# Seven products instead of eight in two FFN up projections of a two-block transformer kernel

## The chip, the cores and the metric

One core of a Trainium2 chip runs the whole kernel in one launch. The metric is device time in microseconds (us); a kernel's time is the median of its runs. The traces come from one profiled execution each. The engines are named as in the profile: PE (TensorE), PEld (its weight loads), DVE (VectorE), ACT (ScalarE), POOL (GpSimd) and SP (the queue that issues most transfers).

## The reference

Two blocks work on one sequence of 1024 tokens with a model width of 1024, all in float32. The part that matters here is the FFN of each block, whose hidden width is 4096: an up projection, the square of a relu, a down projection.

```python
y = x @ w_out                                    # mixer output, 1024 x 1024
x = x + rms_norm(y, mix_post_norm)
h = rms_norm(x, ffn_pre_norm)
f = jnp.square(jax.nn.relu(h @ w_up))            # 1024 x 4096
x = x + rms_norm(f @ w_down, ffn_post_norm)
```

The second block does the same with w_out_2, w_mlp_in_2 and w_mlp_out_2; its norms and sums are scaled and shifted by a modulation, a vector of 6144 numbers that one matrix (w_ada_2, 1024 x 6144) makes of a condition vector. That matrix is 25 MB, and its product is computed beside the first FFN.

## The kernel before, in words

A float32 product is made of three matmuls. Each operand is split into a rounded part (hi, a copy on ACT) and the rest (lo, a subtraction on DVE), and `mm3` (L170) adds hi·hi, hi·lo and lo·hi in one PSUM bank. A weight block of 128 x 128 stands still, 512 tokens stream: these are the 128x512 matmuls of L172.

The stage before each FFN is `out_projection`: it computes the mixer output in two halves of 512 tokens. Behind each half, for each tile of 128 tokens, `epilogue` adds the residual, and `norm_to_hT` norms the tile, transposes it on PE (L283) and writes hi and lo of the transposed activations h, 8 blocks of 128 features by 1024 tokens.

`ffn_up` then goes through the 4096 hidden columns in 16 slabs of 256. `w_cols` loads a slab's weights (1 MB, one raw buffer), casts them (L202) and subtracts (L208) into w_hi and w_lo, of which there are two buffers each. For each half of the tokens and each 128 columns there is one product over all 8 feature blocks: 2 x 2 x 8 x 3 = 96 matmuls. ACT takes relu out of PSUM (L977) and squares it (L978). The four results of a slab, f11, f12, f21 and f22 (half, column block), are combined by DVE into five sums (L993), and these and f11 and f22 go to memory in HBM (fs_dr). The down projection reads them from there: it is already computed by seven Strassen products, its weight sums made on POOL (L1034).

Beside the first `ffn_up` runs the modulation. `modulation_acc` loads a 512-column strip of w_ada_2 in four chunks of 512 KB, issued from POOL's queue (L1095), and adds them up on DVE with the condition vector's entries as scalars (L1099, L1101). There are 12 strips, so 48 chunks.

The program text gives dependences; a scheduler that simulates the program with its own costs fixes one order of instructions per engine, and each engine runs its order without overtaking. Buffers are named in `TAGS`, where a number behind a star says how many a name has: "fp" holds those of `ffn_up` and the modulation.

```python
"fp": "f00*4 f01*4 f10 f11 fs4 fs5 fs0 fs1 fs6 ada_acc*2 ada_raw*3 f_r",
```

Of the kernel before, what the change touches and what calls it, by code (L numbers as in the profile page):

```python
# [65 lines left out]
def tile_two_blocks(ctx: ExitStack, tc: tile.TileContext, I, out):  # L66
# [90 lines left out]
    mix_dr = scratch("mix", (D, S))  # L157
    fs_dr = [scratch(f"fs{i}", (P, 16 * 512)) for i in range(7)]
# [110 lines left out]
    def norm_to_hT(t, xt, xn, junk, hh, hl, row=None, gain=None, bias=None, tmp_pool=None):  # L269
# [9 lines left out]
        for g in range(2):  # L279
# [4 lines left out]
            if row is not None:  # L284
                split(hh[:, ks, tok], hl[:, ks, tok], pt.rearrange("p (a b) -> p a b", a=4))
            else:
                tm = tmp_pool.tile([P, 4, P], F32, name="hmod")
                for j in range(4):
                    k = 4 * g + j
                    ACT.activation(tm[:, j, :], pt[:, j * P:(j + 1) * P], AF.Identity,  # L290
                                   scale=gain[:, k:k + 1], bias=bias[:, k:k + 1])
                POOL.tensor_scalar(hh[:, ks, tok], tm, 1.0, 1.0, ALU.mult, ALU.mult)  # L292
                DVE.tensor_tensor(out=hl[:, ks, tok], in0=tm, in1=r32(hh[:, ks, tok]), op=ALU.subtract)

    def new_hT(pool):
        return (pool.tile([P, KT, S], F32R, name="h_hi"), pool.tile([P, KT, S], F32R, name="h_lo"))

# [629 lines left out]
    def epilogue(t, y, gbc, ep, xsrc, xdst, nxt, eng=DVE):  # L927
# [11 lines left out]
        if nxt is not None:  # L939
            nxt(t, xt, y, junk)  # L940

    def out_projection(w, src, y, mxp, after, last):
        for half in range(2):
# [9 lines left out]
            for c in range(4):  # L953
                ws = w_cols(w, 256 * c, 256)
                for tt in range(4):
                    ps = mm_tile(256)
                    tok_major(ps, 0, ms[tt], ws)
                    ACT.copy(y[:, 4 * half + tt, 256 * c:256 * (c + 1)], ps)
            res = last() if half else None
            for tt in range(4):  # L960
                after(4 * half + tt)
# [4 lines left out]
    def ffn_up(h, w_up, fp, first, side=lambda c: None):  # L966
        NC = w_up.shape[1] // 256
        fs, uw = {}, dict(enumerate(first))

        def up(c, half):  # L970
            if c not in uw:
                uw[c] = w_cols(w_up, 256 * c, 256)
            for j in range(2):
                ps = mm_tile()
                feat_major(ps, j * P, halves[half], h, uw[c])
                f = fs[c, half, j] = fp.tile([P, 512], F32, name=f"f{half}{j}")
                ACT.activation(f, ps, AF.Relu)  # L977
                ACT.activation(f, f, AF.Square)  # L978
                if half == 0 or j == 1:
                    if half != j:  # L980
                        continue
                    left(c, 2 if half == 0 else 3, f, ACT)
# [4 lines left out]
        def sums(c):  # L987
            f11, f12, f21, f22 = (fs.pop((c, half, j)) for half in range(2) for j in range(2))
            for i, x, z, op, eng in ((4, f11, f12, ALU.add, DVE), (5, f21, f11, ALU.subtract, DVE),
                                     (0, f11, f22, ALU.add, DVE), (1, f21, f22, ALU.add, DVE),  # L990
                                     (6, f12, f22, ALU.subtract, DVE)):
                t = fp.tile([P, 512], F32, name=f"fs{i}")
                eng.tensor_tensor(out=t, in0=x, in1=z, op=op)  # L993
                left(c, i, t)


        with tc.high_priority(offset=100):
            up(0, 0), up(1, 0)
        up(2, 0)
        del uw[0]  # L1000
        for c in (2, 1, 0):
            up(c, 1)
            sums(c)
            side(2 - c)
        for c in range(3, NC):
            up(c, 0), up(c, 1)
            sums(c)
            side(c)
# [346 lines left out]
    with sbuf("hT", 1) as hp:  # L1355
        h = new_hT(hp)
# [96 lines left out]
```

## Time and profile before

| | |
|---|---|
| median of 3 runs | 2799.05 us (2797.68 to 2800.49) |
| profiled execution | 2806.41 us, span 2804.7 us |
| granted TensorE clock, mean | 0.988 |
| PE busy | 2705.9 us, 96% of the span, 14184 matmuls |
| DVE, ACT, POOL busy | 1656.2 (59%), 1209.2 (43%), 607.5 us (22%) |
| HBM | 385.76 MB read, 138.20 MB written, 187 GB/s over the span |

The span runs from the first to the last instruction of the profiled execution. The rows are shown below, ahead of the prediction. In them "x" counts instructions, `out<-in` names the tiles, and a bracket at the end of a timeline row says how long the engine sat idle before it, and for whom.

### The profile page before, as it was taken

The page shows a single profiled execution, that of the slowest core. Times are in us where ns is not written, and L with a number is a line of the kernel's source. Part 1 is how long each engine was busy: PE and PEld are TensorE (multiplying, and loading weights), DVE is VectorE, ACT ScalarE, POOL GpSimd, SP SyncE. Part 2 cuts the span into 40 slices and gives each one's busy share as a digit, 9 for nine tenths or more (in the row PEclk, how much of TensorE's full clock was granted, in tenths as well). Part 3 has the DMA queues.
Part 4 walks back from the last instruction along what each step waited for, and adds up shares of the span by engine and source line. Part 5 has one row for each costly group of instructions (what it writes and reads, how often), then busy time and mean ns, then how long its engine had stood idle before and what let it go on. Part 6 is the DMA issues. An engine that isn't in the chain of part 4 may idle for free. (4 is left out here: it accounts for less than half of the span.)

```text
span 2804.7 us, 39229 instructions
## 1 busy us (share of the span) xinstructions
PE 2705.9 (96%) x14184; PEld 2297.1 (82%) x14184; DVE 1656.2 (59%) x3137; ACT 1209.2 (43%) x2207; POOL 607.5 (22%) x600
## 2 busy tenths in 40 slices
PE   7999989999999999999899999999999999999996
PEld 7788879999777788877798888887798888888785
DVE  7678689858644335568632258776566322245665
ACT  5544666545333334345521146564265333343342
POOL 1242344212111021424200022112212000023413
PEclk9999999999999999999999999999999999999998
DMA  4286576446876456777441445434765544467775
GB/s 131 80 289 203 155 208 179 123 156 220 279 253 224 158 193 222 267 260 268 142 152 61 164 152 158 119 107 158 243 211 190 172 139 132 148 220 254 259 275 187
DMA packets 344744, 526.56 MB, mean 188 GB/s; under 512 B 37491, under 2 KB 191194, under 8 KB 344550
## 3 DMA queue, kind: packets, MB, share of 16 engines
q1 hardware_dynamic: 328422, 482.10, 52.4%
q0 software_dynamic: 6912, 25.17, 2.6%
q10 hardware_dynamic: 9216, 16.78, 1.7%
q8 instruction: 112, 1.84, 0.3%
q14 instruction: 82, 0.67, 0.1%
HBM read 385.76 MB, written 138.20 MB: 187 GB/s over the span
## 5 line engine op out<-in xcount | busy, mean ns | idle before, releaser
L172 PE MATMUL mm<-h_hi,w_hi 128*128 128x512 f32 x1760 | 689.7, 393 | 1.4 <-POOL h_hi L292 1.4
L172 PE MATMUL mm<-h_lo,w_hi 128*128 128x512 f32 x1760 | 688.8, 391 | 0.0
L172 PE MATMUL mm<-h_hi,w_lo 128*128 128x512 f32 x1760 | 687.4, 391 | 0.0
L172 PE MATMUL mm<-w_hi,df 128*128 128x512 f32 x1792 | 556.3, 391 | 3.6 <-DVE y L1067 1.7
L172 PEld LDWEIGHTS mm<-w_hi,df 128*128 128x128 f32 x1792 | 337.6, 188 | 75.6 <-DVE y L1067 2.7
L172 PEld LDWEIGHTS mm<-h_hi,w_hi 128*128 128x128 f32 x1760 | 330.7, 188 | 78.8 <-ACT w_hi L202 7.8
L172 PEld LDWEIGHTS mm<-h_hi,w_lo 128*128 128x128 f32 x1760 | 330.9, 188 | 66.9
L172 PEld LDWEIGHTS mm<-h_lo,w_hi 128*128 128x128 f32 x1760 | 331.0, 188 | 66.0 <-issue 0.2
L172 PE MATMUL mm<-w_lo,df 128*128 128x512 f32 x896 | 350.9, 392 | 7.2 <-DVE w_lo L178 7.2
L208 DVE TENSOR_TENSOR w_lo<-w_raw,w_hi 128x1024 fp32r<-128x1024 f32 (+1 forms) x182 | 225.9, 1267 | 181.9 <-ACT w_hi L202 179.5
L202 ACT CAST w_hi<-w_raw 128x1024 fp32r<-128x1024 f32 (+1 forms) x182 | 182.3, 1048 | 281.6 <-PE mm L172 187.5
L993 DVE TENSOR_TENSOR fs<-f,f 128x512 f32<-128x512 f32 x160 | 106.9, 702 | 247.2 <-ACT f L978 226.7
L178 DVE TENSOR_TENSOR df<-dfr,df 128x1024 fp32r<-128x1024 f32 x112 | 153.5, 1383 | 100.6 <-ACT df L177 100.5
L977 ACT ACTIVATE f<-mm 128x512 f32<-128x512 f32 x128 | 76.4, 597 | 300.6 <-PE mm L172 273.8
L172 PEld LDWEIGHTS mm<-w_lo,df 128*128 128x128 f32 x896 | 168.8, 188 | 45.3 <-DVE w_lo L178 10.5
L1034 POOL TENSOR_TENSOR w_raw<-w_raw 128x1024 f32<-128x1024 f32 x40 | 108.3, 2708 | 403.8 <-DMA fs<-f 357.8
L172 PE MATMUL mm<-w_hi,mixT 128*128 128x256 f32 x1024 | 185.7, 283 | 3.7 <-DVE m_sg L1285 1.6
L1034 POOL TENSOR_TENSOR dwr<-dwr 128x1024 f32<-128x1024 f32 x40 | 102.4, 2559 | 384.2 <-DMA dwr<-in_w_mlp_out 214.5
L177 ACT CAST df<-dfr 128x1024 fp32r<-128x1024 f32 x112 | 115.7, 1050 | 119.4 <-PE mm L172 74.7
L172 PEld LDWEIGHTS mm<-w_hi,mixT 128*128 128x128 f32 x1024 | 158.3, 190 | 5.7 <-ACT mixT L177 2.1
L178 DVE TENSOR_TENSOR w_lo<-dwr,w_hi 128x1024 fp32r<-128x1024 f32 x56 | 96.8, 1728 | 104.4 <-ACT w_hi L177 104.0
L172 PE MATMUL mm<-w_lo,mixT 128*128 128x256 f32 x512 | 144.2, 282 | 3.6 <-DVE w_lo L208 3.6
(354 smaller groups left out, 4512.9 us busy)
## 6 DMA issues: line engine op xcount, KB each, us to landing
dfr<-fs SPq DMA_DIRECT2D x112, 512.0 KB
fs<-fs SPq DMA_DIRECT2D x160, 256.0 KB
w_raw<-in_w_in SPq DMA_DIRECT2D x32, 1024.0 KB
ada_raw<-in_w_ada POOLq DMA_DIRECT2D x48, 512.0 KB, 7.4
dwr<-in_w_down SPq DMA_DIRECT2D x48, 512.0 KB
w_raw<-in_w_down SPq DMA_DIRECT2D x48, 512.0 KB
dwr<-in_w_mlp_out SPq DMA_DIRECT2D x48, 512.0 KB
w_raw<-in_w_mlp_out SPq DMA_DIRECT2D x48, 512.0 KB
```

What stands on the lines that cost most here:

```text
L172: PE.matmul(ps, l, r, start=first and n == 0, stop=final and n == last)
L177: ACT.copy(hi, src)
L178: DVE.tensor_tensor(out=lo, in0=src, in1=r32(hi), op=ALU.subtract)
L202: ins = ACT.copy(wh[:, step * i:step * i + step], raw[:, step * i:step * i + step])
L208: DVE.tensor_tensor(out=wl[:, c], in0=raw[:, c], in1=r32(wh[:, c]), op=ALU.subtract)
L977: ACT.activation(f, ps, AF.Relu)
L993: eng.tensor_tensor(out=t, in0=x, in1=z, op=op)
L1034: POOL.tensor_tensor(out=a, in0=a, in1=b, op=ALU.subtract if sub else ALU.add)
```

## The change

Both up projections are computed by seven Strassen products per slab in place of eight. The feature blocks and the 256 columns are cut in two each, which makes four weight quarters a11, a12, a21 and a22 (column block, feature half); the activations are cut into four quarters too, b11 and b21 (the first token half, feature halves 1 and 2), b12 and b22 (the second token half). Seven products of combined quarters, each over 4 feature blocks (12 matmuls), give f11, f12, f21 and f22.

- The weight sums s1 to s4 are made by POOL from the raw slab and split like weights (`slab`, new L1059 to L1080). They and the plain quarters fill both buffers of w_hi and w_lo.
- The token sums t1 to t4 and b22 are made when the epilogue of tiles 4 to 7 hands over its transposed tile (`Quarters.put`, new L326 to L356): for each tile, 5 quarters are written, hi and lo.
- Two of the seven products need first-half tokens only (a11·b11 and a12·b21). For slabs 0 to 7 (`LEAD = 8`) they are computed between the first token half and the end of the second half's epilogue, with weights that are loaded once more for it, written to HBM (fx_dr) and read back by the slab. Such a slab has 5 products left, the others 7.
- DVE adds the products out of PSUM (7 additions per slab). Relu and square both read SBUF. The five sums for the down projection move from DVE to POOL.
- Buffers: ada_raw goes from three to two, ada_acc from two to one, the f tiles to one or two each.
- The activations h of the second block and some pools of the stages around it lie elsewhere in memory.

```diff
-    "fp": "f00*4 f01*4 f10 f11 fs4 fs5 fs0 fs1 fs6 ada_acc*2 ada_raw*3 f_r",
+    "fp": "fws fx*2 f00*2 fu2 fu3 f01 f10 f11 fs*3 ada_acc ada_raw*2 f_r",
...
+        def put(self, t, g, src, tmp, in_psum):
...
+            (b12, w), b22 = self.held.pop(t), src
...
+            DVE.tensor_tensor(out=w[:, 2], in0=b22, in1=b12, op=ALU.subtract)
+            DVE.tensor_tensor(out=w[:, 0], in0=b12, in1=h11, op=ALU.subtract)
+            POOL.tensor_tensor(out=w[:, 0], in0=w[:, 0], in1=l11, op=ALU.subtract)
+            ACT.copy(th[:, 0, :, tok], b22)
+            DVE.tensor_tensor(out=tl[:, 0, :, tok], in0=b22, in1=r32(th[:, 0, :, tok]), op=ALU.subtract)
+            DVE.tensor_tensor(out=w[:, 1], in0=b22, in1=w[:, 0], op=ALU.subtract)
+            POOL.tensor_tensor(out=w[:, 3], in0=w[:, 1], in1=h21, op=ALU.subtract)
+            POOL.tensor_tensor(out=w[:, 3], in0=w[:, 3], in1=l21, op=ALU.subtract)
+            ACT.copy(th[:, 1:4, :, tok], w[:, 0:3])
+            DVE.tensor_tensor(out=tl[:, 1:4, :, tok], in0=w[:, 0:3], in1=r32(th[:, 1:4, :, tok]), op=ALU.subtract)
+            ACT.copy(th[:, 4, :, tok], w[:, 3])
+            DVE.tensor_tensor(out=tl[:, 4, :, tok], in0=w[:, 3], in1=r32(th[:, 4, :, tok]), op=ALU.subtract)
...
-        def up(c, half):
...
-                ACT.activation(f, ps, AF.Relu)
-                ACT.activation(f, f, AF.Square)
...
-            for i, x, z, op, eng in ((4, f11, f12, ALU.add, DVE), (5, f21, f11, ALU.subtract, DVE),
...
+        def slab(c, lead):
+            raw = wp.tile([P, 2112], F32, name="w_raw", tag="w_raw", bufs=1)[:, :2048]
+            SP.dma_start(raw.rearrange("p (k n) -> p k n", k=8),
+                         w_up[:, 256 * c:256 * c + 256].rearrange("(k p) n -> p k n", p=P))
...
+            for o, x, z, op in ((s1, a21, a22, ALU.add), (s2, s1, a11, ALU.subtract), (s3, a11, a21, ALU.subtract),
+                                (s4, a12, s2, ALU.subtract)):
+                POOL.tensor_tensor(out=o, in0=x, in1=z, op=op)
...
+            if not lead:
+                halves_of(u[0], slice(2, 4), r4[:, :, 0])
+            halves_of(u[0], slice(0, 2), ws[:, 0:2])
+            halves_of(u[1], slice(0, 2), ws[:, 2:4])
+            halves_of(u[1], 2, a22)
+            if lead:
+                x, f11 = (fp.tile([P, 512], F32, name=nm) for nm in ("fx", "f00"))
+                for i, t in enumerate((x, f11)):
+                    SP.dma_start(t, fx_dr[:, 512 * (2 * c + i):512 * (2 * c + i) + 512])
+                q2 = f11
+            else:
+                x = p1(fp, op(u[0], 2))
+            q6 = mm_tile()
+            product(q6, op(u[0], 0), "t2")
+            u2 = fp.tile([P, 512], F32, name="fu2")
+            DVE.tensor_tensor(out=u2, in0=x, in1=q6, op=ALU.add)
+            if not lead:
+                q2 = mm_tile()
+                product(q2, op(u[0], 3), "b21")
+                f11 = fp.tile([P, 512], F32, name="f00")
+            DVE.tensor_tensor(out=f11, in0=x, in1=q2, op=ALU.add)
+            square(f11)
+            left(c, 2, f11, ACT)
...
+            for i, x, z, o, eng in ((4, f11, f12, ALU.add, POOL), (0, f11, f22, ALU.add, POOL),
...
+        with tc.high_priority(offset=100):
+            for c in range(LEAD):
...
+                    product(acc, a, b)
+                    x = fl.tile([P, 512], F32, name=("fx", "f00")[i])
+                    ACT.copy(x, acc)
+                    ACT.dma_start(fx_dr[:, 512 * (2 * c + i):512 * (2 * c + i) + 512], x)
+        for c in range(NC):
+            slab(c, c < LEAD)
             side(c)
```

Three places of the order follow. The first is POOL's order in the first FFN: in the kernel before, from the last gate product of the mixer over the 8 tiles of the epilogue (yg) and the modulation's issues to the down projection's weight sums (dwr, w_raw).

```order
L795 TENSOR_TENSOR g_knT_7542<-g_knT_7542,g_gate 128x512
L935 TENSOR_TENSOR yg<-y,gpost 128x1024 x8
L1095 DMA ada_raw<-in_w_ada 128x2x512 x5
L1034 TENSOR_TENSOR dwr<-dwr 128x1024
L1095 DMA ada_raw<-in_w_ada 128x2x512 x43
L1034 TENSOR_TENSOR w_raw<-w_raw 128x1024
```

In the changed kernel, where slabs 2 to 3 are worked on (fws are the weight sums, fs the sums for the down projection):

```order
L1067 TENSOR_TENSOR fws<-w_raw 128x512 x2
L1067 TENSOR_TENSOR fws<-fws,w_raw 128x512
L1229 DMA ada_raw<-in_w_ada 128x2x512
L1067 TENSOR_TENSOR fws<-w_raw,fws 128x512
L1125 TENSOR_TENSOR fs<-f_10075,f_10125 128x512
L1229 DMA ada_raw<-in_w_ada 128x2x512
L1125 TENSOR_TENSOR fs<-f_10075,f_10143 128x512
L1125 TENSOR_TENSOR fs<-f_10143,f_10125 128x512
L1229 DMA ada_raw<-in_w_ada 128x2x512
L1125 TENSOR_TENSOR fs<-f_10147,f_10075 128x512
L1125 TENSOR_TENSOR fs<-f_10147,f_10125 128x512
L1067 TENSOR_TENSOR fws<-w_raw 128x512 x2
```

The issues stood in two runs of 5 and 43 with one weight sum of the down projection between; now they stand one by one between the sums of the slabs.

The second place is DVE's order where the epilogue ends and the slabs begin. Before, with the last tiles' activations (h_lo) and the first modulation sums:

```order
L178 TENSOR_TENSOR h_lo<-tr,h_hi 128x4x128
L276 SCALAR_TENSOR_TENSOR y<-xt,nrsy,grow 128x1024
L178 TENSOR_TENSOR h_lo<-tr,h_hi 128x4x128
L1099 TENSOR_SCALAR ada_acc<-ada_raw,vec 128x512
L1101 SCALAR_TENSOR_TENSOR ada_acc<-ada_raw,vec,ada_acc 128x512 x5
L178 TENSOR_TENSOR h_lo<-tr,h_hi 128x4x128 x2
L1101 SCALAR_TENSOR_TENSOR ada_acc<-ada_raw,vec,ada_acc 128x512
L993 TENSOR_TENSOR fs_9419<-f_9330,f_9359 128x512
```

In the changed kernel, from the first slab's weight subtraction (w_lo<-fws) over the sums of the last two tiles (htt, hq_t) to the last tile's last subtraction:

```order
L179 TENSOR_TENSOR w_lo<-fws,w_hi 128x1024
L354 TENSOR_TENSOR hq_t_8909<-htt,hq_t_8908 128x12x128
L356 TENSOR_TENSOR hq_t_8909<-htt,hq_t_8908 128x4x128
L345 TENSOR_TENSOR htt<-tr,htt 128x512
L346 TENSOR_TENSOR htt<-htt,hq_7678 128x512
L1097 TENSOR_TENSOR f_9500<-fx,f_9500 128x512
L179 TENSOR_TENSOR w_lo<-fws,w_hi 128x1024
L179 TENSOR_TENSOR w_lo<-w_raw,w_hi 128x512
L1097 TENSOR_TENSOR f_9640<-fx,f_9640 128x512
L349 TENSOR_TENSOR hq_t_8909<-tr,hq_t_8908 128x4x128
L350 TENSOR_TENSOR htt<-tr,htt 128x512
L354 TENSOR_TENSOR hq_t_8909<-htt,hq_t_8908 128x12x128
```

The last tile's five steps (from `htt<-tr,htt` behind hq_t of the tile before) now have the weight subtractions of slab 0's second buffer among them.

The third place is PE's order there in the changed kernel, where the last tile's 8 transposes (tr) stand (hq are the first-half quarters, hq_t the second-half ones).

```order
L173 MATMUL mm<-hq_7680,w_hi 128x512
L284 MATMUL tr<-cst,y_3_7725 128x128 x8
L173 MATMUL mm<-hq_7681,w_hi 128x512
L173 MATMUL mm<-hq_7680,w_lo 128x512
L173 MATMUL mm<-hq_7680,w_hi 128x512
L173 MATMUL mm<-hq_7681,w_hi 128x512
L173 MATMUL mm<-hq_7680,w_lo 128x512
L173 MATMUL mm<-hq_t_8908,w_hi 128x512
```

Behind the transposes stand five matmuls of the products ahead, and then the first that reads a quarter of the second half.

## Rows read from the trace of the kernel before

**Rows 1.** Part 1 of the page: busy us, share, instructions of each engine.

```profile
PE 2705.9 (96%) x14184; PEld 2297.1 (82%) x14184; DVE 1656.2 (59%) x3137; ACT 1209.2 (43%) x2207; POOL 607.5 (22%) x600
```

**Rows 2.** Windows: stretch, us, PE, PEld, DVE, ACT, POOL busy, PEclk, DMA share, GB/s.

```profile
660.00:1010.00 350.00, 350.00 (x1523) 278.14 (x1522) 182.02 (x280) 124.29 (x191) 45.38 (x53) 1.00 0.64 219
720.00:760.00 40.00, 40.00 (x172) 31.16 (x171) 22.99 (x31) 15.36 (x23) 5.79 (x8) 1.00 0.82 291
2113.00:2465.00 352.00, 350.62 (x1565) 290.18 (x1565) 117.98 (x180) 129.79 (x208) 23.59 (x17) 1.00 0.48 157
```

**Rows 3.** Waits of PE's matmuls, 555 to 1010 and 2070 to 2480: us, times, longest.

```profile
PE mm L172 <- ACT mixT L177: 1.3, 2, 1.1
...
PE mm L172 <- POOL h_hi L292: 1.4, 1, 1.4
```

**Rows 4.** PE timeline, end of the first up projection: start us, us, what.

```profile
1019.79 0.39 PE L172 MATMUL mm<-h_hi,w_hi 128*128 128x512 f32 x1
...
1025.23 0.39 PE L172 MATMUL mm<-h_hi,w_hi 128*128 128x512 f32 x1
```

**Rows 5.** Durations ns min/median/max and one timeline row: ACT, DVE and POOL elementwise work.

```profile
L177 ACT CAST mixT<-mixR x32: 604/619/624, 558.8 to 2076.3; 128x512 fp32r<-128x512 f32 x32
...
L202 ACT CAST w_hi<-w_raw x182: 893/1050/1108, 9.9 to 2424.6; 128x1024 fp32r<-128x1024 f32 x178, 128x848 fp32r<-128x848 f32 x4
...
L208 DVE TENSOR_TENSOR w_lo<-w_raw,w_hi x182: 1029/1219/3432, 10.8 to 2425.9; 128x1024 fp32r<-128x1024 f32 x178, 128x848 fp32r<-128x848 f32 x4
...
L993 DVE TENSOR_TENSOR fs<-f,f x160: 678/685/1879, 702.2 to 2471.8; 128x512 f32<-128x512 f32 x160
...
850.16 1.89 DVE L993 TENSOR_TENSOR fs<-f,f 128x512 f32<-128x512 f32 x3
...
L1289 POOL TENSOR_TENSOR m_sg<-m_sg,m_sg x16: 1282/1505/2270, 1937.5 to 2025.2; 128x512 f32<-128x512 f32 x16
```

**Rows 6.** Timeline of POOL and DVE at two places: start us, us, what [idle before].

```profile
1950.27 1.23 DVE L208 TENSOR_TENSOR w_lo<-w_raw,w_hi 128x1024 fp32r<-128x1024 f32 x1 [3.15 <-ACT w_hi L202]
...
1951.41 0.68 DVE L1285 TENSOR_TENSOR m_sg<-m_sg,mm 128x512 f32<-128x512 f32 x1
...
1952.01 1.22 DVE L208 TENSOR_TENSOR w_lo<-w_raw,w_hi 128x1024 fp32r<-128x1024 f32 x1
...
1952.22 2.16 POOL L1289 TENSOR_TENSOR m_sg<-m_sg,m_sg 128x512 f32<-128x512 f32 x1 [3.68 <-DVE m_sg L1285]
...
1953.14 0.68 DVE L1288 TENSOR_TENSOR m_sg<-m_sg,mm 128x512 f32<-128x512 f32 x1
...
2758.14 2.40 POOL L1034 TENSOR_TENSOR w_raw<-w_raw 128x1024 f32<-128x1024 f32 x1
...
2759.15 2.47 DVE L178 TENSOR_TENSOR w_lo<-dwr,w_hi 128x1024 fp32r<-128x1024 f32 x1 [3.97 <-ACT w_hi L177]
```

**Rows 7.** Timeline of SP's issues and ACT's casts of up-projection weights.

```profile
644.78 0.38 SPq L197 DMA_DIRECT2D w_raw<-in_w_up  x1
...
650.13 2.00 ACT L202 CAST w_hi<-w_raw 128x1024 fp32r<-128x1024 f32 x2 [1.78 <-DMA w_raw<-in_w_up]
...
715.68 0.38 SPq L197 DMA_DIRECT2D w_raw<-in_w_up  x1
...
724.92 2.00 ACT L202 CAST w_hi<-w_raw 128x1024 fp32r<-128x1024 f32 x2 [6.71 <-DMA w_raw<-in_w_up]
```

**Rows 8.** Tile ada_raw, 680 to 960: durations, idle before by releaser, waits, landing.

```profile
L1101 DVE SCALAR_TENSOR_TENSOR ada_acc<-ada_raw,vec,ada_acc x84: 736/752/2176, 691.8 to 924.3; 128x512 f32<-128x512 f32 x84
...
L1095 POOL DMA_DIRECT2D ada_raw<-in_w_ada x48: 724/724/931, 686.5 to 917.6; - x48
...
  DMA ada_raw<-in_w_ada: 13.7, 9
...
  POOL ada_raw L1095: 190.4, 44
...
DMA to landing us min/median/max: 4.4/7.4/9.0
```

More of the change, by code (lines that the diff above doesn't have):

```diff
@@ L939, in epilogue, with out_projection @@
         if nxt is not None:
-            nxt(t, xt, y, junk)
-    def out_projection(w, src, y, mxp, after, last):
+            nxt(t, xt, y, junk if spare else y)
+    def out_projection(w, src, y, mxp, after, last, between):
         for half in range(2):
@@ L957, in out_projection @@
                     tok_major(ps, 0, ms[tt], ws)
-                    ACT.copy(y[:, 4 * half + tt, 256 * c:256 * (c + 1)], ps)
+                    ACT.copy(y(4 * half + tt)[:, 256 * c:256 * (c + 1)], ps)
             res = last() if half else None
+            if half:
+                between()
             for tt in range(4):
@@ L962, in out_projection @@
         return res
-    def ffn_up(h, w_up, fp, first, side=lambda c: None):
-        NC = w_up.shape[1] // 256
-        fs, uw = {}, dict(enumerate(first))
-        def up(c, half):
[L971 to L976, printed above, removed]
-                ACT.activation(f, ps, AF.Relu)
-                ACT.activation(f, f, AF.Square)
[L979 to L982, printed above, removed]
+    LEAD = 8
@@ L1354, in tile_two_blocks, with stage @@
     w_in2 = I["w_in_2"][0]
[L1355 to L1370 removed]
+    def stage(es, *a, **kw):
+        return es.enter_context(sbuf(*a, **kw))
@@ new lines, in up_stage, with between @@
+    def up_stage(n, w_out, src, mxp, mx_es, w_up, epi, tags, gains, side=lambda fp: lambda c: None):
+        hqx, tx, loc = ExitStack(), ExitStack(), ExitStack()
+        hq = Quarters(stage(hqx, f"hq{n}", 1))
+        fl = stage(hqx, f"fl{n}", 1, tags="fx f00")
+        y1p = stage(loc, f"y1{n}", 1, tags="y1_0 y1_1 y1_2 y1_3")
+        ep = stage(loc, f"ep{n}", 1, tags=tags)
+        y0 = stage(mx_es, f"y0{n}", 1, side="right").tile([P, 4, D], F32, name="y0")
+        y1 = [y1p.tile([P, D], F32, name=f"y1_{i}") for i in range(4)]
+        ys = lambda t: y0[:, t] if t < 4 else y1[t - 4]
+        gains(ep)
+        def between():
+            mx_es.close()
+            hq.second(stage(tx, f"hqt{n}", 1, side="right"))
+        first = out_projection(w_out, src, ys, mxp, lambda t: epi(t, ys(t), ep, hq.put),
+                               lambda: lead_w(w_up, 0), between)
+        loc.close()
+        with sbuf(f"fp{n}", 1, tags=TAGS["fp"]) as fp:
+            ffn_up(hq, w_up, fl, fp, first, side(fp))
+        hqx.close()
+        tx.close()
@@ L1371, in tile_two_blocks, with gains1, side1 @@
+    with ExitStack():
+        with banks(mm=6, tr=2):
+            rows = {}
+            def gains1(ep):
+                for nm, v in (("gpost", "mix_post_norm"), ("grow", "ffn_pre_norm")):
+                    rows[nm] = ep.tile([P, D], F32, name=nm)
+                    bcast_row(rows[nm], I[v][0], D)
+            def side1(fp):
                     pend = {}
@@ L1397, in tile_two_blocks @@
                     pass
+            htx.close()
             late.enter_context(banks(mm=6, tr=2))
```

169 lines of the change are left out of this document (119 added, 50 removed).

## The prediction

> **What bounds the kernel now.** I read the page's busy shares first: TensorE (PE) is busy 2705.9 of 2804.7 us, 96%, and no other engine passes 59% [rows 1]. An average over the program says nothing on one stage, so the windows over both FFN up projections came next: PE is busy in all 350 us of the first and in 350.6 of 352 us of the second, at a granted clock of 1.00, which is the level of 2.4 GHz; VectorE (DVE) is busy 182 and 118 us, ScalarE (ACT) 124 and 130, GpSimd (POOL) 45 and 24 [rows 2]. The waits of PE's matmuls confirm it: the largest sum is 1.3 us up to the end of the first stretch and 1.4 around the second [rows 3]. So these two stages cost what their matmuls cost. On the PE timeline 24 matmuls of 128x512 stand between the starts at 1019.79 and 1025.23, so one takes 5.44 / 24 = 0.2267 us (the 0.39 us of a row overlaps with its neighbours) [rows 4]. 1536 of them, an up projection, are 348.2 us.
>
> The span is 2804.7 us and the profiled execution 2806.41 us, 7.4 above the median 2799.05 of the runs. I add up differences in the trace and subtract them from the median.
>
> **Part A, the matmuls removed.** A slab of 256 columns had 2 halves x 2 column blocks x 8 k x 3 = 96 matmuls; seven products of half the depth are 7 x 4 x 3 = 84. Twelve less in each of 16 slabs and 2 FFNs: 384 x 0.2267 = **-87.0 us**, if PE stays fed. The rest is the question of what feeds it. PE now needs 84 x 0.2267 = 19.04 us for a full slab, and for one of the eight slabs with two products ahead (a lead slab) 60 x 0.2267 = 13.60, against 21.8 before.
>
> **What is added per slab.** POOL gets 4 sums of weights and 5 of products, nine 128x512 additions, of 1.28 us by the shortest POOL row of that shape [rows 5]: 11.5 us per slab where POOL did none. DVE gives up the five sums (0.69 each) and gets 7 additions from PSUM of 0.68. ACT casts as before and squares from SBUF. In a lead slab there is also one raw weight load more per two slabs, and 512 KB of kept products are stored and read back.
>
> POOL and DVE are not independent. In the trace a DVE subtraction with two SBUF inputs that takes 1.23 us by itself took 2.47 beside a POOL addition that had begun 1.01 before it; a POOL addition took 2.16 beside such a DVE subtraction, while a DVE addition with one input in PSUM, begun inside it, kept its 0.68 [rows 6]. So of a slab's work I add, on one lane, POOL's nine sums and DVE's operations with two SBUF inputs: in a lead slab two subtractions of 128x1024 and two operations of 128x512. Back to back these follow each other at 1.14 us (1950.27 to 1951.41 [rows 6]) and 0.63 (three sums in 1.89 [rows 5]). 11.5 + 2.28 + 1.26 = 15.1 us against PE's 13.60. A full slab: 11.5 + 3 x 1.14 + 0.63 = 15.6 against 19.04, covered. The Trainium skill states this as a rule (SBUF — State Buffer, "Who interferes with whom": a DVE instruction with two SBUF inputs contends with a GpSimd one that reads SBUF, one with at most one SBUF input doesn't). The trace agrees, 2.47 against 1.23 and 0.68 unchanged. By the rule the lane costs a lead slab 1.5 us, without it POOL's 11.5 alone would cost nothing.
>
> **Part B, the seam.** In the change's DVE order the sums for the last token tile stand behind the first slab's weight subtractions, and in PE's order the last transposes have five matmuls behind them (1.1 us) before the first that reads the tile's combined quarter. The tile's chain, by nearest rows: copy 0.62, subtractions 0.68 + 0.68, POOL 1.28, DVE 0.68, then a cast and a subtraction of 128x1536, drawn on from the rows of 512 and 1024 columns to 1.5 and 1.76: 7.2 us [rows 5]. Before, the same place in the second FFN cost PE a wait of 1.4 us [rows 3]. Less 1.1 of matmuls, plus the 1.2 + 0.6 of weight subtractions queued ahead on DVE and one or two lock waits of 1.2: about 10 us per FFN. Bounds 5 (the chain alone, partly under matmuls) and 15 (each DVE step meets a POOL sum). I take **+20 us** for both, bounds +10 and +30. The earlier tiles' chains lie beside the products ahead, 192 x 0.2267 = 43.5 us of matmuls, and cost nothing; without that cover it would be the same 7 us for each of three tiles.
>
> **Part C, lead slabs of the second FFN.** Besides the lane of 15.1 us there is a loop through the one raw buffer: subtraction from it, load, POOL's first sums, cast and subtraction. The load took 5.35 us from issue at 644.78 to cast at 650.13, and 9.24 at 715.68 to 724.92 [rows 7]. From the release of the second weight buffer to the last read of raw: a cast 1.05, two subtractions 1.23 + 0.63 and 0.5 of an addition ahead of them, 3.4. Behind the load three sums 3.85, a cast 1.05 and a subtraction 1.23 [rows 5]. The loop is 3.4 + 5.35 + 3.85 + 2.28 = 14.9 us, close to the lane. I take 15.0 for each: 8 x (15.0 - 13.6) = **+11 us**. Bounds: 0 (the queue evens it out over full slabs) and, with the load at 7.4, (14.9 + 2.05 - 13.6) x 8 = +27. Full slabs are PE-bound: 0.
>
> **Part D, the first FFN, where the modulation's weights come in.** 48 chunks of 512 KB are issued from POOL's queue, 0.72 us each, land 7.4 us later (4.4 to 9.0), and are added up by two DVE operations of 0.75 [rows 8]. Before, there were three buffers, and nothing of consequence behind the issues on POOL: it waited 190.4 us for DVE there, 44 times [rows 8], and PE lost next to nothing. Now there are two buffers, and the issues stand in POOL's order between the weight sums that PE waits for. An issue whose buffer is not free holds all sums behind it. The loop of two buffers: 0.72 + 7.4 + 1.5 + about 0.9 of queueing on DVE (half a subtraction's wait) = 10.5 us for two chunks. 46 chunks stand ahead of the weight sums of the slab with index 13: 23 turns, 241.5, and 5 to begin, 246.5 us for 13 slabs. PE alone: 8 x 13.6 + 5 x 19.04 = 204. So **+42.5 us**. Bounds: at 9.6 (nothing queues) 226, +22; below that if landings are faster, to 0 (4.4 to land: 7.5 a turn, hidden); at landings of 9.0, 12.1 a turn, 283.6, +79.6. I take the median landing, since the nearest loaded stretch, 720 to 760, already moved 291 GB/s at a DMA share of 0.82 [rows 2], and lead slabs ask about as much: 1 MB of weights, 1.75 of sums out, 0.5 back and 1.5 of chunks, in some 17 us.
>
> Other moves are small. The down projection's first transfers must wait for memory that the up projection's operands held: 0 to +3 us. The second block's gate matmuls stand otherwise in the order: between -5 and +5, taken as 0.
>
> **Sum:** -87.0 + 20 + 11 + 42.5 = -13.5; 2799.05 - 13.5 = **2786 us**, faster by 0.5%. Its own range, from the bounds of D at turns of 10 to 11 and of B: 2770 to 2805.
>
> **The rivals.**
> *The cover holds.* With landings under 7 us the two-buffer loop hides, and the first FFN's lead slabs cost what the second's do, +11. -87 + 20 + 11 + 11 = -45: 2754 us. For it: DVE found its chunk not yet landed only 9 times, 13.7 us in all [rows 8]. Against: that was with a third buffer.
>
> *The lane decides in the first FFN.* Two modulation additions per chunk have two SBUF inputs, 1.5 us a chunk. Three chunks in a lead slab make 15.1 + 4.5 = 19.6, four in a full one 15.6 + 6 = 21.6; 8 x 19.6 + 5 x 21.6 = 265 against the 246.5 of the loop, +18 on the forecast: 2804, no real gain. For it: [rows 6]. Against: not every addition meets another.
>
> *Slower: issues block the sums.* POOL is in order. At a landing of 9.0 a turn is 12.1 us, D is +79.6, and the sum is -87 + 20 + 11 + 79.6 = +23.6: 2823 us. It decides from a turn of (87 - 31 + 204 - 5) / 23 = 11.1 us upwards, that is with landings above 8.0. For it: 9.0 did occur, and 9.24 for a load on the other queue [rows 7, 8]. Against: the median.
>
> *No sums saved at all.* If the order kept 96 matmuls a slab nothing would be gained; the instruction counts exclude it (12 less per slab).
>
> **How the numbers follow.** Forecast 0.33, cover holds 0.25, lane 0.16, slower 0.26. I call within 0.2% (5.6 us, about what a measurement of this kernel can tell) the same. The forecast's range puts about 0.27 of 0.33 under 2793, the lane 0.03; with the 0.25 that makes faster 0.55. Same: 0.04 + 0.09 = 0.13. Slower: 0.02 + 0.04 + 0.26 = 0.32. The range, 2748 to 2835, leaves out about one in ten at each end: below a cover that also has a short seam, above turns over 12.5.
>
> **What would show it.** A: 24 PE starts still 5.44 us apart where PE is fed, 2688 matmuls in the two stages. B: PE idle some 10 us once in each stage, ended by a DVE write of the token quarters. C: second FFN's lead slabs 15.0 us apart, full slabs 19.0. D: in the first FFN PE waits that end with a subtraction of weights or a cast, POOL idle before its issues for a buffer, lead slabs and full slabs alike some 19 us apart up to the slab with index 12, and 19.0 from there. Wrong would be: first-FFN lead slabs at 14 to 15 us (cover), PE waits without POOL idle before issues but with stretched sums of 2 us and more (lane), landings of 8 us and more (slower), or a PE idle time in a place named nowhere above.

## The result, and the profile after

The changed kernel takes 2919.68 us (median of 4 runs), the kernel before 2799.77 in the same session: a ratio of 1.044 (95% interval 1.040 to 1.048). It is slower by 4.4%, and the prediction, 2786 us with a range to 2835, is wrong in sign.

Part 1 of the page, which answers to [rows 1]: busy us, share of the span, instructions.

```profile
PE 2702.0 (92%) x13800; PEld 2252.3 (77%) x13800; DVE 1918.8 (65%) x3293; ACT 1293.5 (44%) x2335; POOL 1071.5 (36%) x904
```

PE has 384 matmuls fewer and is busy for 4 us less, yet the span is 131 us longer, 2935.9 against 2804.7. The profiled execution took 2937.58 us and the three others 2917 to 2921, so a difference taken against its trace can come out up to 18 us larger in sum than the difference of the medians. DVE and POOL are busier by 263 and 464 us. On the PE timeline I cut the run at the first matmul of each stage; "ahead" are the products computed ahead, "slabs" what follows from the first product of a second-half quarter to the down projection:

| stage, us | before | forecast | after |
|---|---|---|---|
| first output projection | 100.6 | 100.6 | 114.6 |
| first up projection: ahead + slabs | 366.4 | 375.4 | 65.6 + 370.8 |
| first down projection | 319.6 | 319.6 | 330.8 |
| second up projection: ahead + slabs | 353.7 | 331.2 | 64.6 + 316.9 |
| second down projection to the end | 337.5 | 337.5 | 347.3 |

The windows over these stages, columns as in [rows 2], first, up and down projections:

```profile
671.00:1108.00 437.00, 361.01 (x1409) 272.40 (x1408) 336.83 (x360) 166.19 (x254) 273.09 (x204) 0.90 0.60 199
...
2207.00:2588.00 381.00, 333.99 (x1379) 260.79 (x1377) 206.27 (x263) 169.39 (x269) 238.19 (x157) 0.94 0.49 162
...
1108.00:1439.00 331.00, 316.68 (x1376) 257.74 (x1377) 205.62 (x223) 145.31 (x183) 124.75 (x55) 0.98 0.74 257
...
2588.00:2935.00 347.00, 314.50 (x1344) 255.96 (x1344) 213.07 (x223) 132.32 (x149) 117.99 (x46) 0.95 0.73 253
```

The up projections show two losses. PE is idle for 76 and 48 us, where it had none. And its granted clock is 0.90 and 0.94 on average, between the levels of 1.2 and 2.4 GHz: some 87 us of the first stage and 46 of the second stand at the lower one (0.10 x 2 x 437, 0.06 x 2 x 381), in stretches around its waits, where before there was none. At the pace and clock of before PE's work would be 1344 x 0.2267 = 304.7 us and the 18.2 and 5.5 that stood beside the matmuls before, 322.9 and 310.2; PE is busy 360 and 334 us, 37 and 24 more. Of that 6.3 us in each are a slower pace at full clock (part A below); 24 and 9 are 112 and 44 matmuls that start 0.44 us apart without a wait between them; the rest, mostly the last matmul ahead of each wait, is not split. The idle time is thus paid 1.2 to 1.4 times.

The largest waits of PE in the two stretches (engine, line waited for: us, times, longest), the first 735 to 1110, then 2207 to 2590:

```profile
PE mm L173 <- ACT w_hi L178: 32.2, 6, 13.1
PE mm L173 <- DVE w_lo L179: 15.9, 7, 4.3
PE mm L173 <- ACT hq_t L348: 7.6, 1, 7.6
PE mm L1242 <- DVE ada_acc L1235: 6.6, 3, 2.3
...
PE mm L173 <- ACT w_hi L178: 13.2, 11, 2.7
...
PE mm L173 <- ACT hq_t L348: 11.4, 1, 11.4
...
PE mm L173 <- ACT hq_t L353: 7.4, 1, 7.4
```

They end with casts and subtractions of weights, `w_hi` and `w_lo`, and at the seam with the second-half quarters (`hq_t`), 7.6 us in the first FFN, 11.4 + 7.4 in the second. In the first FFN the modulation's own matmuls (L1242) wait as well, for DVE's sum of the chunks.

### The profile page after: what moved, and what is told of

It reads as the page before. It is cut to its first block, busy times and chain, and to the rows that moved or that the text cites. A ratio compares the mean times of both kernels' runs of the same rounds, so it can differ in the third digit from the quotient of the medians.

```text
span 2935.9 us, 39406 instructions
## 1 busy us (share of the span) xinstructions
PE 2702.0 (92%) x13800; PEld 2252.3 (77%) x13800; DVE 1918.8 (65%) x3293; ACT 1293.5 (44%) x2335; POOL 1071.5 (36%) x904
## 4 chain that ended last, share of the span: by engine, by line
PE 25%; DMA 12%; DVE 7%; POOL 5%; issue 3%; ACT 3%; SPq 0%; ACTq 0%; POOLq 0%; DVEq 0%
PE mm L173 21%; DMA w_raw<-in_w_mlp_in 4%; DVE w_lo L179 3%; POOL fws L1067 2%; DMA dwr<-in_w_mlp_out 2%; ACT w_hi L178 1%; PE po L903 1%; DMA w_raw<-in_w_mlp_out 1%; PE tr L895 1%; POOL dwr L1168 1%; DVE w_lo L209 1%; DMA mixR<-mrg 1%; DMA w_raw<-in_w_down 1%; DMA m_sg<-sig 1%; POOL w_raw L1168 1%
## 5 line engine op out<-in xcount | busy, mean ns | idle before, releaser
L173 PE MATMUL mm<-hq_t,w_hi 128*128 128x512 f32 x1280 | 420.7, 414 | 74.8 <-ACT w_hi L178 43.2
L173 PEld LDWEIGHTS mm<-hq_t,w_hi 128*128 128x128 f32 x1280 | 251.0, 198 | 151.8 <-ACT w_hi L178 52.8
L173 PE MATMUL mm<-w_lo,df 128*128 128x512 f32 x896 | 354.7, 396 | 10.4 <-DVE w_lo L179 10.3
L173 PE MATMUL mm<-h_hi,w_hi 128*128 128x512 f32 x736 | 293.0, 398 | 0.0
L173 PE MATMUL mm<-h_lo,w_hi 128*128 128x512 f32 x736 | 292.5, 397 | 0.0
L173 PE MATMUL mm<-h_hi,w_lo 128*128 128x512 f32 x736 | 291.9, 397 | 0.0
L1125 POOL TENSOR_TENSOR fs<-f,f 128x512 f32<-128x512 f32 x160 | 254.4, 1608 | 86.5 <-ACT f L1048 67.4
L173 PE MATMUL mm<-hq_t,w_lo 128*128 128x512 f32 x640 | 257.3, 411 | 13.2 <-DVE w_lo L179 13.0
L179 DVE TENSOR_TENSOR w_lo<-w_raw,w_hi 128x1024 fp32r<-128x1024 f32 (+2 forms) x114 | 150.2, 1322 | 118.6 <-ACT w_hi L178 118.1
L1168 POOL TENSOR_TENSOR dwr<-dwr 128x1024 f32<-128x1024 f32 x40 | 98.8, 2471 | 316.5 <-DMA dwr<-in_w_mlp_out 185.1
L1047 ACT ACTIVATE f<-f 128x512 f32<-128x512 f32 x128 | 80.4, 630 | 217.0 <-DVE f L1107 88.7
L173 PE MATMUL mm<-hq,w_hi 128*128 128x512 f32 x512 | 166.6, 405 | 2.2 <-ACT w_hi L178 2.2
```

The costliest lines, as they stand in the source:

```text
L173: PE.matmul(ps, l, r, start=first and n == 0, stop=final and n == last)
L179: DVE.tensor_tensor(out=lo, in0=src, in1=r32(hi), op=ALU.subtract)
L1047: ACT.activation(f, f, AF.Relu)
L1125: eng.tensor_tensor(out=t, in0=x, in1=z, op=o)
L1168: POOL.tensor_tensor(out=a, in0=a, in1=b, op=ALU.subtract if sub else ALU.add)
```

## Experiments

Theories: **R**, the one raw weight buffer closes a loop that is longer than PE's work on a slab. **L**, POOL's sums and DVE's two-input operations shut each other out, and DVE works in order. **I**, the modulation's issues hold the weight sums in POOL's queue. The table has the traces' stages and the medians; the first two rows are for comparison.

| | output proj. 1 | ahead 1 | slabs 1 | down 1 | ahead 2 | slabs 2 | down 2 | median |
|---|---|---|---|---|---|---|---|---|
| before | 100.6 | | 366.4 | 319.6 | | 353.7 | 337.5 | 2800 |
| after | 114.6 | 65.6 | 370.8 | 330.8 | 64.6 | 316.9 | 347.3 | 2919.7 |
| e1 product sums on DVE | 115.9 | 65.6 | 349.1 | 333.5 | 64.3 | 309.1 | 344.9 | 2910.4 |
| e2 a quarter of the chunks | 115.1 | 65.5 | 318.3 | 328.8 | 64.4 | 316.5 | 340.7 | 2885.1 |
| e3 second raw buffer, FFN 2 | 114.8 | 65.7 | 360.1 | 326.8 | 63.0 | 283.9 | 345.2 | 2881.6 |
| e4 all sums on DVE | 115.9 | 63.1 | 334.2 | 326.9 | 60.2 | 289.8 | 340.1 | 2858.6 |
| e5 a22 in first buffer | 114.9 | 65.3 | 371.9 | 330.5 | 64.6 | 287.9 | 339.3 | 2893.7 |
| e6 e5 + e1 | 114.4 | 65.2 | 345.9 | 334.4 | 65.3 | 296.0 | 342.9 | 2884.5 |
| e7 e6 + 12 ahead | 114.1 | 74.3 | 351.1 | 329.4 | 75.0 | 279.1 | 339.9 | 2888.8 |
| e8 issues, few additions | 114.6 | 65.7 | 346.1 | 328.7 | 64.5 | 315.9 | 343.3 | 2904.8 |
| e9 issues on SP | 115.1 | 65.6 | 363.1 | 327.5 | 64.5 | 317.0 | 347.5 | 2925.4 |
| e10 before, sums on POOL | 102.0 | | 367.2 | 320.1 | | 353.3 | 336.0 | 2799.5 |
| e11 second FFN alone | 101.9 | | 366.3 | 319.8 | 72.8 | 263.9 | 344.0 | 2793.2 |
| e12 e5 + e2 | 115.6 | 65.2 | 301.5 | 323.5 | 65.1 | 288.4 | 339.4 | 2820.0 |
| e13 e11, 16 ahead | 101.9 | | 366.3 | 320.8 | 89.1 | 253.1 | 342.0 | 2797.5 |
| e14 yg on DVE | 101.5 | 63.4 | 372.0 | 328.2 | 64.4 | 318.5 | 342.9 | 2917.0 |

Stages that an edit leaves alone move by up to 11 us in the first slabs (e3) and by 5 to 8 elsewhere; smaller differences carry nothing, and each stage figure is of a single trace. The medians fall by 9.3 us for e1, 34.6 for e2, 38.1 for e3, 61.1 for e4, 26.0 for e5 and 14.9 for e8, where the spans of the traces fall by 15 to 22 more. Totals of e1 to e9, e12 and e14 are of two timed runs each; all lie above the kernel before beyond their intervals. e2, e8 and e12 leave out part of the modulation's work, so they price it and are no versions of the kernel.

**The raw loop (e3, e5).** First what it looks like: the timeline of the changed kernel in one full slab of the second FFN, where slabs are 21.5 us apart (the first two full slabs 19.0 and 19.9):

```profile
2530.37 1.78 DVE L179 TENSOR_TENSOR w_lo<-w_raw,w_hi 128x512 fp32r<-128x512 f32 x1
...
2532.18 0.38 SPq L1059 DMA_DIRECT2D w_raw<-in_w_mlp_in  x1
...
2538.66 3.52 POOL L1067 TENSOR_TENSOR fws<-w_raw 128x512 f32<-128x512 f32 x2 [4.09 <-DMA w_raw<-in_w_mlp_in]
...
2539.69 1.35 DVE L179 TENSOR_TENSOR w_lo<-w_raw,w_hi 128x1024 fp32r<-128x1024 f32 x1 [5.74 <-ACT w_hi L178]
...
2542.16 1.28 POOL L1067 TENSOR_TENSOR fws<-fws,w_raw 128x512 f32<-128x512 f32 x1
...
2543.47 1.05 ACT L178 CAST w_hi<-fws 128x1024 fp32r<-128x1024 f32 x1 [3.82 <-POOL fws L1067]
...
2544.55 1.32 DVE L179 TENSOR_TENSOR w_lo<-fws,w_hi 128x1024 fp32r<-128x1024 f32 x1 [3.51 <-ACT w_hi L178]
...
2544.57 0.74 PE L173 MATMUL mm<-hq_t,w_hi 128*128 128x512 f32 x2 [0.85 <-ACT w_hi L178]
...
2545.93 0.50 PE L173 MATMUL mm<-hq_t,w_lo 128*128 128x512 f32 x1 [0.62 <-DVE w_lo L179]
...
2545.80 0.68 DVE L1107 TENSOR_TENSOR f<-fu,mm 128x512 f32<-128x512 f32 x1
...
2546.50 0.63 ACT L1047 ACTIVATE f<-f 128x512 f32<-128x512 f32 x1 [1.99 <-DVE f L1107]
...
2550.34 0.61 ACT L178 CAST w_hi<-w_raw 128x512 fp32r<-128x512 f32 x1
...
2551.88 1.78 DVE L179 TENSOR_TENSOR w_lo<-w_raw,w_hi 128x512 fp32r<-128x512 f32 x1
...
2553.69 0.38 SPq L1059 DMA_DIRECT2D w_raw<-in_w_mlp_in  x1
```

The raw buffer is loaded at 2532.18, just as DVE's last read of it ends (2530.37 + 1.78), and again at 2553.69, 21.51 later. Between them: the load until POOL starts its sums (6.5), three sums (4.8, the first two stretched beside DVE's 1.35), a cast (1.05), a subtraction (1.32); only then does DVE come to the additions of the slab before, which stand behind it in its order, then ACT's squares of those, and behind them on ACT the casts for the second weight buffer, of which the last reads raw. PE waits twice in each round, 0.85 and 0.62.

```diff
-            raw = wp.tile([P, 2112], F32, name="w_raw", tag="w_raw", bufs=1)[:, :2048]
+            raw = (fp.tile([P, 2048], F32, name="w_rawb") if two and c % 2 == 0 else
+                   wp.tile([P, 2112], F32, name="w_raw", tag="w_raw", bufs=1)[:, :2048])
```

e3 (`two` is true in the second FFN only) was expected to do this:

> A second raw weight buffer for the slabs of the second FFN only. Theory R: full slabs there go from 21.5 us to about 19.8 and lead slabs from 16.5 to about 15, so the second stage falls from 381.5 to about 355. Theory L: the same work is on the lane, a change of 5 us at most. The first stage stays at 436 for all.

The slabs fell by 33.0 us, as R expected. In the windows over full slabs, after first and then e3, PE is idle no more:

```profile
2444.00:2553.00 109.00, 101.39 (x425) 78.34 (x424) 50.17 (x56) 44.95 (x65) 69.16 (x46) 1.00 0.41 133
```

```profile
2425.00:2503.00 78.00, 78.00 (x338) 63.14 (x337) 38.72 (x45) 36.46 (x52) 48.56 (x38) 1.00 0.43 153
```

Full slabs are 19.49 us apart there, lead slabs 15.1 on average. e5 reaches nearly the same without a buffer:

```diff
-            halves_of(u[0], slice(0, 2), ws[:, 0:2])
-            halves_of(u[1], slice(0, 2), ws[:, 2:4])
-            halves_of(u[1], 2, a22)
+            halves_of(u[0], 1, a22)
+            halves_of(u[0], 0, ws[:, 0])
+            halves_of(u[1], slice(0, 3), ws[:, 1:4])
```

> The quarter a22, which is split straight from the raw weights, goes into the first weight buffer of a slab in place of the sum s3, which goes into the second; the products follow. No buffer is added, but the raw buffer is now free when the first weight buffer is filled, and no longer waits for PE to leave the second. From the first product of the second token half to the down projection the changed kernel's trace has 370.8 us in the first FFN and 316.9 in the second. Theory R (raw loop): the second falls to about 285, as with a second raw buffer (283.9), the first by 25 to 40, the whole to about 2855 us. Theory L (lane): the same work stays on POOL and DVE, so the first falls by less than 10.

The second FFN's slabs fell by 29.0 us, as R expected, the first's not at all, and the whole came to 2893.7 for 2855. R holds in the second FFN; in the first something else ends last.

**The modulation in the first FFN (e2, e8, e9, e12).** e2 is `range(1)` in place of `range(4)` over the chunks:

> Three of four chunks of the modulation matrix are left out: 12 issues on POOL and 24 DVE operations are left of 48 and 96. Theory I: the first FFN up stage falls from 436.5 to near the second's, about 390, and POOL's 55 us of waiting before its issues goes to under 10. Theory L expects nearly as much, 395 to 405, since 63 of DVE's two-input operations go, but stretched rows of weight subtractions stay. Theory R: at most 10 us. The second stage stays at 381 for all.

The first slabs fell by 52.5 us, to 318.3, which is near the second FFN's 316.5 in the same trace: the chunks left out account for nearly the whole difference between the two FFNs. e8 keeps the issues and drops the additions alone:

```diff
-            for k in range(2):
+            for k in range(2 if q == 0 else 0):
```

> All 48 chunks of the modulation matrix are loaded by POOL's issues as in the changed kernel, but only the first of each four is added up (24 DVE operations of 96); the other additions are left out. Theory I (issues in POOL's order, and their traffic): the slabs of the first FFN stay within 15 us of 370.8. Theory L (lane, DVE in order): they fall to near the 318.3 that leaving out three of four chunks gave, at most 330.

It fell between both expectations: 24.7 us go with 72 DVE additions, the other 27.8 with 36 issues and the 18.9 MB that they load; with 11 us of scatter in these slabs that is about half each (14.9 and 19.7 by the medians). e9 moves the issues (`SP.dma_start` for `POOL.dma_start`):

> The modulation's chunks are issued from SP's queue in place of POOL's, all else as in the changed kernel (370.8 us in the first FFN's slabs). Theory I (issues in POOL's order, 0.72 us each, hold the weight sums): with none there the slabs fall by the 28 us that the issues and loads were found to cost, to about 345, unless SP's queue, which also loads the weights in order, is held in the same way; then they stay within 10 us or rise. If only the traffic of 25 MB costs, they stay as well, and PE's waits don't change their place.

7.7 us less in the slabs, within what they vary by, and no gain in all. The waits show why it decides little: POOL's wait before its issues in the changed kernel, with the landings, and then SP's in e9 (line, waited for: us, times, longest):

```profile
POOL ada_raw L1229 <- DVE ada_acc L1235: 54.7, 30, 5.0
...
DMA to landing us min/median/max: 4.0/5.2/8.1
```

```profile
SPq L1229 <- DVE ada_acc L1235: 69.9, 36, 6.6
```

The chunks land in 5.2 us, sooner than the 7.4 of [rows 8]; what is waited for is DVE, which reaches the additions late. The wait goes with the issues to whatever queue holds them. Whether issue time or traffic makes up the 27.8 us stays open. e12 joins e5 and e2:

> a22 in the first weight buffer, and three of four chunks of the modulation matrix left out. Each alone left the first FFN's slabs at 371.9 and 318.3 us. If the raw loop stands behind the modulation there as it does in the second FFN, where removing it gave 29 to 33 us, the slabs now fall to about 288, the second FFN's value. If the first FFN has another limit, they stay at 310 to 318.

301.5, between both expectations: another 16.8 us under e2. So the raw loop does stand behind the modulation, but gives 16.8 where it gives 28.1 in the second FFN of the same two traces; the last 13 us to 288.4 stay unsplit.

**The lane (e1, e4, e6, e10).** What L says can be seen in the changed kernel's timeline around 820 us, DVE first, then POOL, then ACT and PE:

```profile
818.67 5.96 DVE L1097 TENSOR_TENSOR f<-fx,f 128x512 f32<-128x512 f32 x1 [2.42 <-DMA f<-fx_dr]
...
817.96 1.25 POOL L1067 TENSOR_TENSOR fws<-fws,w_raw 128x512 f32<-128x512 f32 x1
...
819.17 3.69 POOL L1125 TENSOR_TENSOR fs<-f,f 128x512 f32<-128x512 f32 x3
...
822.83 1.25 POOL L1067 TENSOR_TENSOR fws<-w_raw,fws 128x512 f32<-128x512 f32 x1
...
824.66 0.63 ACT L1047 ACTIVATE f<-f 128x512 f32<-128x512 f32 x1 [6.59 <-DVE f L1097]
...
826.38 1.03 ACT L178 CAST w_hi<-fws 128x1024 fp32r<-128x1024 f32 x1
...
827.47 2.07 PE L173 MATMUL mm<-hq_t,w_hi 128*128 128x512 f32 x4 [13.10 <-ACT w_hi L178]
```

DVE's addition of 128x512, 0.68 us by itself, takes 5.96: it starts inside a POOL sum and ends 0.55 after the last of the four that follow without a gap. ACT has waited 6.59 us for it; behind its relu and square in ACT's order stands the cast of the weights, and PE has waited 13.10 us for that. [rows 6] had shown one such step, not a train. The Trainium skill (SBUF — State Buffer, "Who interferes with whom") calls the port pair that the two engines share an exclusive lock, and its rule names a DVE instruction with two SBUF inputs as one that contends. The trace agrees, and here the addition stood through the rest of one POOL instruction and four whole ones. e1 puts the five product sums back on DVE:

> The five sums per slab for the down projection go back to DVE, the four weight sums stay on POOL. Theory L (lane): POOL's sums and DVE's operations with two SBUF inputs exclude each other, and DVE, in order, is held through trains of POOL sums (their DVE rows are 85 us over their shortest in the first FFN up stage, 22 in the second). It expects the first stage (436.5 us in the trace of the changed kernel) to fall to about 395, the second (381.5) to about 360, the whole to about 2855 us. Theory R (raw loop): the one raw weight buffer, read last by the second weight buffer's subtraction, paces the slabs; the product sums are not in that loop, so both stages move by less than 10 us. Theory I (issues): the modulation's issues in POOL's order hold the weight sums; they stay, so the first stage falls by at most 10 and the second not at all.

21.7 us less in the first slabs, 7.8 in the second: about half and a third of what L expected. The medians differ by 9.3 us only, not much over the 7.8, so the 21.7 is not firm. e4 puts the four weight sums there as well:

> All nine sums of a slab on DVE; POOL has only the modulation's issues and the token sums. Theory L: nothing excludes DVE any more; the second stage falls to about 355 (DVE has 13 us of work in a lead slab), the first to about 400 (17 us of DVE work in a lead slab with the modulation's additions), the whole to about 2860. Theory I: the first falls to about 395 since the issues hold no weight sums, the second stays at 381. Theory R: both stay within 10 us.

It met L's numbers, 397.3 and 350.0 us for the up projections, 2858.6 in all; theory I had expected 395 for the first as well, but 381 for the second. R was not to expect it, since the raw buffer is as before; but full slabs of the second FFN stand 19.49 us apart, the first 21.3. The two theories are not apart: the loop's steps are the very operations that the lane stretches, and short enough they close it within PE's work. One slab of the first FFN still lost 21.7 us in two waits (11.3 and 10.4) of the modulation's matmuls on PE for DVE's sums, which came late. e6, e5 and e1 together, disappointed:

> The edit before, and the five product sums on DVE. Theory L: once the raw loop is gone the lane sets the first FFN's slabs, and five sums at 0.63 on DVE for 1.28 on POOL take 3 us off each: the first stage falls by another 25 to 40 against the edit alone, the second by about 5, the whole to about 2820 us. Theory R alone: nothing more than the edit alone gives.

26.0 us under e5 in the first slabs as expected, 8.1 above it in the second, and the whole came to 2884.5 for 2820: with the loop gone the sums are no better on DVE in the second FFN, and in the first the modulation's matmuls now wait 19.4 us for DVE's sums (4.9 in e5). e10 asks whether the stretching costs by itself: the kernel before with `POOL` for `DVE` in its five sums and `ada_acc ada_raw*2`:

> The kernel before, with two parts of the change alone: its five product sums go from DVE to POOL, and the modulation gets two chunk buffers and one accumulator in place of three and two. Eight products per slab as before. Theory L says the lane of such a slab (6.4 us of sums, 2.3 of weight subtractions, 6 of modulation additions) is well below PE's 21.8 us, so both FFN up stages keep 366 and 354 us to within 5. If the sums on POOL or the two buffers did harm of their own, the first stage would be over 10 us longer.

Ratio 0.9996 (0.9984 to 1.0009). The rows of the modulation's additions and the window over its first up projection:

```profile
L1101 DVE SCALAR_TENSOR_TENSOR ada_acc<-ada_raw,vec,ada_acc x84: 743/752/2089, 666.4 to 955.3; 128x512 f32<-128x512 f32 x84
...
660.00:1027.00 367.00, 366.17 (x1597) 291.68 (x1596) 163.35 (x205) 128.49 (x197) 160.97 (x132) 1.00 0.66 219
```

Of these 84 additions of 0.75 us 26 take over 1 us (one did in the kernel before), up to 2.09, together 26.5 us over the shortest, and PE is busy 366.17 of 367 us. So the stretching costs nothing by itself here. PE has 21.8 us a slab, no weights are summed on POOL, and the weight subtractions on DVE lose 2.5 us in all; which of these makes it free was not tried apart.

**Cover at the seam (e7, e13).** e7 is e6 with `LEAD = 12`:

> The kernel before in this call, with the two products of 12 slabs ahead in place of 8: 96 more matmuls, 21.8 us, stand before the first that needs the second token half. If the last tiles' chain of sums sets the end of that stretch (65.6 and 64.6 us for 43.5 of matmuls ahead), the stretch grows by under 10 us in each FFN and the slabs behind it lose some 18: about 10 us less per FFN. If it is set by the matmuls and their weights, it grows by 20 or more and nothing is won, or 5 us are lost per FFN with the loads and stores that come on top.

Of the 96 matmuls more, 78 and 89 stand ahead of the first that reads a second-half quarter, 17.7 and 20.2 us. They lengthened "ahead" by 9.1 and 9.7 us against e6: some 9 and 10 of idle time were covered, as expected of a stretch that the last tiles' sums end. The second FFN won 7 us in all; the first lost 14: in its slabs PE's waits for weight subtractions rose from 8.3 to 22.0 us and those of the modulation's matmuls for DVE's sums from 19.4 to 27.4.

**The first output projection (e14).** The edit leaves `eng=POOL` out of the first epilogue:

> In the changed kernel the product y times gain of the first FFN's epilogue goes from POOL to DVE, as the second FFN has it. The stage of the first output projection took 114.6 us, 14 more than before, where the second's lost nothing. If DVE's short scalar steps, which stood at 2.35 us beside that POOL product, hold the stage up, it falls to 103 to 108. If it is the shared buffer of the square and the product, it stays at 112 to 117.

114.6 us became 101.5; in the other ten traces of the changed kernel's first output projection it is 114.1 to 115.9. The median, 2917.0 for 2919.7, doesn't show the gain. The cause in the changed kernel, two rows of its timeline:

```profile
613.65 2.36 POOL L995 TENSOR_TENSOR yg<-y,gpost 128x1024 f32<-128x1024 f32 x1 [4.81 <-DVE nrsb L222]
...
613.67 2.35 DVE L226 SCALAR_TENSOR_TENSOR nrsy<-nrsb,nrsy 128x1 f32<-128x1 f32 x1
```

A DVE step on 128x1 numbers, 0.16 us by itself, takes 2.35 beside POOL's product; five such steps of this stage take 2.05 to 2.39, none over 0.5 in e14. In the kernel before, beside the same product, the longest took 0.93. [rows 6] held no such case.

**A version that is faster (e11).** The first FFN as before, the second with e3's buffer and `LEAD = 12`:

> The first FFN as before; the second with seven products, a second raw buffer and 12 slabs ahead. From the runs so far the second up stage should take 75 us for the products ahead and 262 to 270 for the slabs (12 lead slabs of 15.0, the rest of 19.5), 337 to 345 against 353.7 before, with 3 to 8 us lost in the down projection behind it: a total 5 to 12 us under the kernel before, 0.2 to 0.4%. If lead slabs stay at 16.5 us (the raw loop is not what set them), the stage takes 355 or more, and the kernel is no faster than before.

2793.2 us, a ratio of 0.9974 (0.9964 to 0.9985) to the kernel before: 0.26% faster. The up projection takes 336.7 us for 353.7; the down projection gives back 6.5. e13, with all 16 slabs ahead, tried the memory of the first-half quarters as the reason for that:

> The kernel with the first FFN as before and the second with a second raw buffer, with the two products of all 16 slabs ahead in place of 12. The first-half quarters are then read for the last time before the slabs, and the memory that the down projection's first tiles take over is free some 240 us earlier. If it is this memory that delays the down projection (344.0 us against 337.5 before), that stage falls to 338 to 340; if not, it stays at 343 to 346. The products ahead should take 94 us and the slabs 16 x 15.2 = 243, so that the up stage stays at about 337. Total 2788 or 2793.

342.0 against 344.0: not shown, and the up projection took 342.2 us for the 337 expected, and the total is 0.9990 (0.9978 to 1.0001), no gain. Why the down projections are longer stays open; 2.6 and 4.5 us of it are PE's wait for their first tile, which had none before.

## Why the prediction was wrong

- **Part A** counted right, but at 0.2267 us for every matmul. Those that stream a second-half quarter start 0.2333 apart, at a granted clock of 1.00 and without a wait (below): 960 x 0.0066 = 6.3 us per FFN.
- **Part B** had the right place, and 10.3 and 19.9 us of waits there for 10 each, at its upper bound: in the second FFN POOL's sum for the last tile stood behind weight sums that waited 6.8 us for their load. Within the products ahead PE also waited 6.8 and 3.8 us for the earlier tiles' norms ahead of their transposes, which the prediction put at nothing. It left out what such a wait does to the clock. The window over the first seam shows 0.50, the 1.2 GHz level:

```profile
733.00:746.00 13.00, 5.94 (x13) 4.36 (x14) 10.25 (x11) 7.91 (x12) 5.19 (x4) 0.50 0.41 141
```

- **Part C is the step that failed**, in the words "Full slabs are PE-bound: 0" and in 15.0 us for a lead slab. Measured are 21.5 (19.0 and 19.9 for the first two) and 16.9 on average. The raw loop was set up for lead slabs only, with a load of 5.35 and steps at their unstretched times, and without the additions and squares that stand in DVE's and ACT's orders between the first weight buffer's steps and the last read of raw. e3 priced it at 33 us in the second FFN, where the prediction had 11, and e12 at 16.8 in the first, once the modulation is out of the way.
- **Part D** had about the right size, 42.5 against 52.5 by e2 (which keeps a quarter of the chunks), by the wrong mechanism, so that was luck. Landings were 5.2 us, so the loop of two buffers is 0.72 + 5.2 + 1.5 + 0.9 = 8.3 a turn and would have hidden. The additions on the lane and in DVE's order are half of it (e8). The slower rival, landings of 9, did not happen either; of the rivals the lane came nearest, with trains of sums in place of single ones. One more path stood in no part: PE's waits for the modulation's sum, 6.6 us in the changed kernel and 19 to 27 in e4, e6 and e7.
- **The terms were added as if PE's idle time cost only itself.** PE is 37 us busier in the first up projection than its work at full clock, 24 in the second; 6.3 of each is part A's, and 24 and 9 are matmuls at the slower clock. The Trainium skill (TensorE: Matmul & The Clock Gate, "HAM oscillation — how this bites in real kernels") shows this for a kernel that waits for transfers: each of its groups of matmuls starts slow behind the wait. The trace agrees with 0.50 at the seam, though most waits here end with a cast or a subtraction; the prediction left it out.
- **"Other moves are small"** failed by 33 us: 14 in the first output projection, of which e14 gives back 13 in that stage, and 10 to 11 in each down projection, unexplained for the most part.

By stage: 61 us too little in the first up projection, 50 in the second, 33 outside, together 144.7; with the forecast's -13.5 that is the 131.2 by which the spans differ.

## What to carry to other kernels

Before work is taken off the engine that sets the time, write down for every single buffer the loop from its load to its last read, with the instructions that stand between in each engine's order, and compare that with the engine's new, shorter period, not with the old one. Sums moved to a second elementwise engine were free in e10, with slack in every slab, and were not in the changed kernel, where the weights pass through both engines and PE has less time per slab: look for that slack first. And a wait of TensorE is to be priced with the slower clock behind it.

## What the runs showed of the hardware that was not expected

- A DVE operation with two SBUF inputs can be shut out by a whole train of POOL sums: 5.96 us for 0.68. One on 128x1 took 2.35 for 0.16 beside a single POOL product.
- Matmuls of the same shape, 512 columns each, differ by 3% with the tile that they stream. On the PE timeline 30 of them that read `hq` lie between the first two of these rows (6.80 us, 0.2267 each), 12 that read `hq_t` between the last two (2.80, 0.2333):

```profile
2211.90 0.62 PE L173 MATMUL mm<-hq,w_hi 128*128 128x512 f32 x2
...
2218.70 0.62 PE L173 MATMUL mm<-hq,w_hi 128*128 128x512 f32 x2
...
841.20 0.63 PE L173 MATMUL mm<-hq_t,w_hi 128*128 128x512 f32 x2
...
844.00 0.63 PE L173 MATMUL mm<-hq_t,w_hi 128*128 128x512 f32 x2
```

The activations of the second block, which the change puts elsewhere in memory, do the same (from 0.228 to 0.233 from start to start on average). That the place in memory is the cause was not tried.
